# The third and fourth weight sums of a group are written over the loaded block that they are the last to read

## The chip, the cores and the metric

The kernel runs on one core of one Trainium2 chip. The metric is the device time of one execution in microseconds, taken as the median of repeated runs. TensorE (PE) does the matrix products, VectorE (DVE) and ScalarE (ACT) the element work, GpSimd (POOL) a little of it, and SyncE (SP) issues nearly all loads.

## The reference, cut to what matters

One decoder layer on 256 tokens of width 1024: three attention mixers, a gated merge, a layer norm, then a feed-forward part. The change lies in the second product of the feed-forward part, `w_down`, with 4096 rows of 1024:

```python
x = layer_norm(ALPHA * x + merged @ w_out[i], ln1_g[i], ln1_b[i])
h = jnp.square(jax.nn.relu(x @ w_up[i])) @ w_down[i]
ple = jax.nn.sigmoid(x @ w_ple_gate[i]) * (p[i] @ w_ple[i])
x = layer_norm(ALPHA * x + h + ple, ln2_g[i], ln2_b[i])
```

## The kernel before, in words

**A block and its split.** Weights come in blocks of 128 x 1024 fp32 (512 KB). `Weights._split` loads a block into a `raw` buffer (SP, L71), ACT casts it to a high part `whi` (L75), and DVE subtracts that to get the low part `wlo` (L79). TensorE then takes three products per tile, in `prod`: high by high (L133), with `wlo` (L134), and with the low part of the activations (L135). There are five `raw` buffers and five pairs of `whi` and `wlo`. A load waits on SP's queue until its `raw` buffer is free, that is until the last reader of the tile that held it has ended.

**The down product.** 16 of the 32 row blocks of `w_down` are multiplied plainly (here p1 to p16, read from `wdn`, 12 products of 512 columns each). The other 16 form four groups (`quad(u)`, QUADS = 4) by a scheme with seven products instead of eight. Each group loads three blocks a, c, d and a sum t1. The sum t1 is loaded into a tile called `rows` by a plain load from SP (L728) and a second load from POOL that adds to it (L729). From these DVE makes t2 = t1 + c, t3 = t2 - a and t4 = t2 + d in `make` (L752). All seven are split and multiplied like any block, with 6 products of 512 columns each. Here t4 of group 2 is called t4(2), and so on.

**Order.** TensorE takes the units in this order, which a loop writes out (three units of the groups, then a plain block):

```
a1 t1(1) c1 p1 | t2(1) t3(1) d1 p2 | t4(1) a2 t1(2) p3 | c2 t2(2) t3(2) p4 | d2 t4(2) a3 p5
t1(3) c3 t2(3) p6 | t3(3) d3 t4(3) p7 | a4 t1(4) c4 p8 | t2(4) t3(4) d4 p9 | t4(4) p10 ... p16
```

Each engine works through its own queue in a fixed order that a scheduler sets when the kernel is built. So on DVE the making of t2 stands in line with the splits, and a making of t2 whose c has not landed holds up every split behind it. Before, t2 has a buffer of its own (pool `p3`), and t3 and t4 each take one of the five `raw` buffers.

**The end.** The last six plain blocks go to five accumulators one after the other: b0, b4 and b1 (512 columns each), then b3 and b2 (256 each). As each is finished, DVE adds it to the rest (L833 before, L834 in the changed kernel), takes statistics (L605), and normalises (L617, L619). `rs` comes from POOL (L612).

Of the kernel before, what the change touches and what calls it, by code (L numbers as in the profile page):

```python
# [11 lines left out]
F32 = mybir.dt.float32  # L12
# [81 lines left out]
def hybrid_layer(ctx: ExitStack, tc: tile.TileContext, x0, xn, pT, wqk, wva, wvb, wg, wbc, wba,  # L94
# [5 lines left out]
    raw = ctx.enter_context(tc.tile_pool(name="raw", bufs=5))  # L100
# [26 lines left out]
    t = banks.tile([128, 512], F32, name="b4", tag="b4")  # L127
# [39 lines left out]
    for t in TASKS:  # L167
# [4 lines left out]
        elif t in "gcao":  # L172
            u, w, n = {"g": (u_g, wg, 1024), "c": (u_bc, wbc, 640), "a": (u_ba, wba, 768),
                       "o": (u_out, wout, 1024)}[t]
# [250 lines left out]
    for j in range(4):  # L425
# [3 lines left out]
        for h in range(2):  # L429
            act.activation(r[:, h], s[h], AF.Relu)  # L430
            for b in range(2):
                n = 2 * j + h
# [38 lines left out]
    for j in range(3):  # L471
# [5 lines left out]
        for h in range(2):  # L477
            n = 2 * j + h
# [9 lines left out]
    for j in range(3):  # L488
# [3 lines left out]
        for h in range(2):  # L492
            n = 2 * j + h
# [91 lines left out]
    p3 = ctx.enter_context(tc.tile_pool(name="p3", bufs=1, reuse_waits="tile"))  # L585
# [57 lines left out]
    for b in range(2):  # L643
        t = slice(b * 128, (b + 1) * 128)
# [31 lines left out]
    for f in range(32):  # L676
# [21 lines left out]
        if m % 2 == 0:  # L698
            continue
        hi, lo, y = ((hQ[:, u, 0, 0], hQ[:, u, 0, 1], g[:, 0, 0:2]) if m == 1 else  # L700
                     (hQ[:, u, 1:3, 0], hQ[:, u, 1:3, 1], g[:, :, 2:4]))
# [23 lines left out]
    def first_sum(u):  # L725

        if u < QUADS:
            nc.sync.dma_start(pair[:, u % 2], wdq[u, 1])  # L728
            pool.dma_start(pair[:, u % 2], wdq[u, 0], accum_op=ALU.add)  # L729
# [6 lines left out]
    def quad(u):  # L736

        t = {}

        def load(n):  # L740
            t[n] = raw.tile([128, 1024], F32, name="raw", tag="raw")
            nc.sync.dma_start(t[n], wdq[u, "abcd".index(n)])
            return t[n]

        def have():
            t["t1"] = pair[:, u % 2]
            return t["t1"]

        def make(n, x, y, f):
            p = p3 if n == "t2" else raw  # L750
            t[n] = p.tile([128, 1024], F32, name="raw", tag="raw")
            dve.tensor_tensor(t[n], t[x], t[y], op=f)  # L752
            if n == "t2":
                first_sum(u + 2)
            return t[n]

        A = [(hQ[:, u, m, 0], hQ[:, u, m, 1]) for m in range(3)]
        Z = sums[u]
        return [(lambda: load("a"), A[0], "P1"), (have, Z[0], "P5"),
                (lambda: load("c"), Z[3], "12"),  # L760
                (lambda: make("t2", "t1", "c", ALU.add), Z[1], "P6"),
                (lambda: make("t3", "t2", "a", ALU.subtract), Z[2], "P7"),
                (lambda: load("d"), A[1], "11"),
                (lambda: make("t4", "t2", "d", ALU.add), A[2], "21")]
# [189 lines left out]
```

## Time and profile before

| | |
|---|---|
| median of 3 runs | 448.35 us (447.51 to 448.59) |
| the profiled execution: time | 447.16 us |
| the profiled execution: span | 445.4 us |
| PE busy in the span | 428.7 us (96%) |
| DVE, ACT, POOL busy | 339.7, 272.7, 104.5 us |
| granted TensorE clock, mean | 0.996 |

The profile was taken on one execution; its own time is 1.8 us longer than the span of its instructions. A busy PE is not PE at its peak: products are pipelined, and each is shown from its start to its modelled end, so two in a row overlap. The distance from start to start says more.

### The profile page before, as it was taken

How to read it: one execution, taken by the hardware profiler on the slowest of the kernel's cores; microseconds unless marked ns; L12 is line 12 of the kernel's file. 1: busy time of each engine (PE TensorE's matmuls, PEld its weight loads, DVE VectorE, ACT ScalarE, POOL GpSimd, SP SyncE). 2: the span in 40 equal slices, each digit the busy share in tenths (PEclk: the TensorE clock that was granted, in tenths of full speed). 3: DMA queues.
4: the chain of work that ended last, by engine and by line, in shares of the span. 5: the costliest groups of instructions: out<-in, count | busy, mean ns of one | idle time of the engine just before them, and what ended most of it. 6: DMA issues, size and time to landing. Idle time of an engine off the chain costs nothing.

```text
span 445.4 us, 7749 instructions
## 1 busy us (share of the span) xinstructions
PE 428.7 (96%) x2833; PEld 386.8 (87%) x2833; DVE 339.7 (76%) x608; ACT 272.7 (61%) x491; POOL 104.5 (23%) x103
## 2 busy tenths in 40 slices
PE   7999999998999999999999999999999999899992
PEld 7989999998999989999886888888888888678882
DVE  4978977446545578759958779999987978779966
ACT  6765465576777748857605567778885865564600
POOL 2654256388533546500001000000000000000001
PEclk9999999999999999999999999999999999999998
DMA  8896855539634336459860866556793658457702
GB/s 290 297 325 181 255 176 182 157 114 302 204 110 141 125 88 198 135 175 330 278 242 1 294 211 192 190 185 203 248 282 115 164 188 237 148 182 243 277 0 95
DMA packets 27722, 86.38 MB, mean 194 GB/s; under 512 B 2928, under 2 KB 6936, under 8 KB 27300
## 3 DMA queue, kind: packets, MB, share of 16 engines
q1 hardware_dynamic: 25872, 79.54, 54.0%
q0 software_dynamic: 672, 2.16, 2.8%
q10 hardware_dynamic: 1140, 4.19, 2.7%
q8 instruction: 22, 0.36, 0.3%
q14 instruction: 16, 0.13, 0.1%
HBM read 83.98 MB, written 1.90 MB: 193 GB/s over the span
## 4 chain that ended last, share of the span: by engine, by line
PE 54%; DVE 8%; DMA 6%; issue 5%; ACT 1%; POOL 1%; POOLq 0%; DVEq 0%; SPq 0%
PE mm L681 10%; PE mm L133 7%; PE mm L134 7%; PE mm L135 7%; DMA raw<-in_wdq_dram 6%; PE b L134 5%; PE b L135 5%; PE mm L683 5%; PE b L133 5%; DVE wlo L79 4%; PE b L271 1%; DVE raw L752 1%; DVE r L686 1%; ACT whi L75 1%; DVE st L605 1%
## 5 line engine op out<-in xcount | busy, mean ns | idle before, releaser
L75 ACT CAST whi<-raw 128x1024 fp32r<-128x1024 f32 (+3 forms) x146 | 146.6, 1012 | 82.0 <-issue 17.9
L79 DVE TENSOR_TENSOR wlo<-raw,whi 128x1024 fp32r<-128x1024 f32 (+5 forms) x146 | 156.2, 1083 | 38.6 <-ACT whi L75 34.9
L79 POOL TENSOR_TENSOR wlo<-raw,whi 128x384 fp32r<-128x384 f32 (+3 forms) x58 | 76.5, 1325 | 84.8 <-ACT whi L75 72.9
L133 PE MATMUL mm<-xh,whi 128*128 128x256 f32 x336 | 95.0, 283 | 1.0 <-DVE G L251 1.0
L135 PE MATMUL mm<-xh,wlo 128*128 128x256 f32 x336 | 95.5, 284 | 0.0
L134 PE MATMUL mm<-xl,whi 128*128 128x256 f32 x336 | 94.7, 282 | 0.0
L133 PEld LDWEIGHTS mm<-xh,whi 128*128 128x128 f32 x336 | 63.3, 188 | 1.5 <-DVE G L251 1.2
L681 PE MATMUL mm<-x,whi 128*128 128x512 f32 x256 | 64.1, 392 | 0.0
L135 PEld LDWEIGHTS mm<-xh,wlo 128*128 128x128 f32 x336 | 63.3, 188 | 0.8
L134 PEld LDWEIGHTS mm<-xl,whi 128*128 128x128 f32 x336 | 63.3, 188 | 0.3
L681 PEld LDWEIGHTS mm<-x,whi 128*128 128x128 f32 x256 | 46.1, 189 | 8.3
L683 PEld LDWEIGHTS mm<-x,wlo 128*128 128x128 f32 x256 | 34.9, 190 | 2.5
L683 PE MATMUL mm<-x,wlo 128*128 128x256 f32 x256 | 35.7, 282 | 0.0
L729 POOL DMA_DIRECT2D rows<-in_wdq_dram x4 | 3.5, 880 | 131.4 <-DMA rows<-in_wdq_dram 131.4
L134 PE MATMUL b<-wlo,hT 128*128 128x512 f32 (+1 forms) x82 | 31.5, 385 | 1.9 <-DVE wlo L79 1.9
L135 PE MATMUL b<-whi,hT 128*128 128x512 f32 (+1 forms) x82 | 31.1, 380 | 0.0
L612 POOL TENSOR_TENSOR rs<-rs,half 128x1 f32<-128x1 f32 x4 | 4.1, 1030 | 111.4 <-DVE rs L611 111.4
L133 PE MATMUL b<-whi,hT 128*128 128x512 f32 (+1 forms) x82 | 27.5, 379 | 0.0
L686 DVE TENSOR_REDUCE r<-mm 128x256 f32<-128x512 f32 x32 | 22.0, 687 | 4.5 <-PE mm L683 4.5
L134 PEld LDWEIGHTS b<-wlo,hT 128*128 128x128 f32 x82 | 15.4, 188 | 6.3 <-DVE wlo L79 3.6
L687 ACT ACTIVATE r<-r 128x256 f32<-128x256 f32 x32 | 13.3, 416 | 10.0 <-DVE r L686 10.0
L134 PE MATMUL mm<-op,whi 128*128 128x256 f32 x64 | 18.0, 282 | 0.0
(198 smaller groups left out, 813.9 us busy)
## 6 DMA issues: line engine op xcount, KB each, us to landing
raw<-in_wup_dram SPq DMA_DIRECT2D x32, 512.0 KB
raw<-in_wg_dram SPq DMA_DIRECT2D x24, 512.0 KB
raw<-in_wqk_dram SPq DMA_DIRECT2D x18, 512.0 KB
raw<-in_wdn_dram SPq DMA_DIRECT2D x16, 512.0 KB
raw<-in_wdq_dram SPq DMA_DIRECT2D x12, 512.0 KB
raw<-in_wout_dram SPq DMA_DIRECT2D x8, 512.0 KB
raw<-in_wpg_dram SPq DMA_DIRECT2D x8, 512.0 KB
T<-tabd SPq DMA_DIRECT2D x24, 128.0 KB
```

The lines of the kernel that those rows point to most:

```text
L75: nc.scalar.copy(hi, r)
L79: e.tensor_tensor(lo[:, c], r[:, c], hi[:, c].bitcast(F32), op=ALU.subtract)
L133: pe.matmul(ps, lhsT=a[0], rhs=b[0], start=first, stop=False)
L134: pe.matmul(ps, lhsT=a[0], rhs=b[1], start=False, stop=False)
L135: pe.matmul(ps, lhsT=a[1], rhs=b[0], start=False, stop=last)
L271: m = pe.matmul(ss[h][:, QC[b]], lhsT=q[d, x, c], rhs=k[d, y, 0:128 * (b + 1)], start=i == 0, stop=i == 2)
L605: dve.bn_stats(st[b][:, c], y)
L681: pe.matmul(ps, lhsT=hi[:, cs[k]], rhs=x1[:, :, k], start=k == 0, stop=False)
L683: pe.matmul(ps[:, :, 0], lhsT=lo[:, cs[k]], rhs=x1[:, :, k, 0], start=False, stop=k == KT - 1)
L686: dve.tensor_reduce(r, ps.rearrange("p b a t -> p b t a"), axis=AX.X, op=ALU.add)
L687: act.activation(r, r, AF.Relu)
L752: dve.tensor_tensor(t[n], t[x], t[y], op=f)
```

## The change

In `make`, t3 and t4 no longer take a new `raw` buffer. The output is the tile `t[y]` that the sum is the last to read: t3 is written over a, t4 over d. Only t2 still gets a tile of its own, as before.

```diff
         def make(n, x, y, f):
-            p = p3 if n == "t2" else raw
-            t[n] = p.tile([128, 1024], F32, name="raw", tag="raw")
+            t[n] = t[y]
+            if n == "t2":
+                t[n] = p3.tile([128, 1024], F32, name="raw", tag="raw")
             dve.tensor_tensor(t[n], t[x], t[y], op=f)
```

The group stage now takes 28 `raw` buffers in turn instead of 36: eight sums no longer take one. t3 has to wait until a has been cast and split, t4 until d has been. The lines after this place move down by one (L752 is L753, L833 is L834). The number of instructions, loads and products is the same; what moves is which release each load waits for, and the order on DVE, ACT and PE.

By the semaphore counts in the two built programs, these loads wait for these instructions:

| load | before: waits for the end of | after: waits for the end of |
|---|---|---|
| d1 | the split of the last `w_up` block | the split of the `w_up` block before it |
| c2 | the split of d1 | the split of t3(1), which stands in a1's buffer |
| d2 | the making of t3(2) | the split of t4(1) |
| c3 | the split of p4 | the split of t3(2), which stands in a2's buffer |
| d3 | the making of t3(3) | the split of t4(2) |
| a4 | the split of p6 | the split of c3 |
| c4 | the split of t3(3) | the split of p6 |

First place: DVE's queue at the seam of groups 2 and 3, before. In the names, raw_4657 is d2, raw_4669 t4(2), raw_4721 c3, raw_4733 t2(3), raw_4681 a3, raw_4763 t3(3), raw_4693 p5, and rows_4458 t1.

```order
L79 TENSOR_TENSOR wlo_4660<-raw_4657,whi_4659 128x1024
L79 TENSOR_TENSOR wlo_4672<-raw_4669,whi_4671 128x1024
L752 TENSOR_TENSOR raw_4733<-rows_4458,raw_4721 128x1024
L79 TENSOR_TENSOR wlo_4684<-raw_4681,whi_4683 128x1024
L752 TENSOR_TENSOR raw_4763<-raw_4733,raw_4681 128x1024
L79 TENSOR_TENSOR wlo_4696<-raw_4693,whi_4695 128x1024
L79 TENSOR_TENSOR wlo_4712<-rows_4458,whi_4711 128x1024
```

The same place after. Here raw_4654 is d2 and then t4(2), raw_4717 c3, raw_4729 t2(3), raw_4677 a3 and then t3(3), raw_4689 p5.

```order
L79 TENSOR_TENSOR wlo_4657<-raw_4654,whi_4656 128x1024
L753 TENSOR_TENSOR raw_4654<-raw_4611,raw_4654 128x1024
L753 TENSOR_TENSOR raw_4729<-rows_4458,raw_4717 128x1024
L79 TENSOR_TENSOR wlo_4668<-raw_4654,whi_4667 128x1024
L79 TENSOR_TENSOR wlo_4680<-raw_4677,whi_4679 128x1024
L79 TENSOR_TENSOR wlo_4692<-raw_4689,whi_4691 128x1024
L753 TENSOR_TENSOR raw_4677<-raw_4729,raw_4677 128x1024
```

The making of t4(2) moved from earlier in the queue to behind d2's split, and t4(2)'s split now stands behind the making of t2(3), where it stood ahead of it.

Second place: PE's queue shortly before the accumulators b0, b4, b1 are finished, before. b3_5026 is accumulator b3.

```order
L133 MATMUL b1_4539<-whi_4991,hT_2959 128x512
L133 MATMUL b3_5026<-whi_4949,hT_2959 128x256
L134 MATMUL b3_5026<-wlo_4950,hT_2959 128x256
L135 MATMUL b3_5026<-whi_4949,hT_2959 128x256
L134 MATMUL b0_4532<-wlo_4992,hT_2959 128x512
```

The same place after (b3_5018 is b3; the L133 and L134 of its first block stand further up).

```order
L133 MATMUL b1_4538<-whi_4983,hT_2959 128x512
L135 MATMUL b3_5018<-whi_4941,hT_2959 128x256
L133 MATMUL b3_5018<-whi_4953,hT_2959 128x256
L134 MATMUL b3_5018<-wlo_4954,hT_2959 128x256
L135 MATMUL b3_5018<-whi_4953,hT_2959 128x256
L134 MATMUL b0_4531<-wlo_4984,hT_2959 128x512
```

Six products of b3 now stand ahead of the last ones of b0, b4 and b1; before there were three.

Third place: DVE's queue in the final normalisation, before.

```order
L605 BN_STATS st_5100<-Y_3172 128x6
L619 SCALAR_TENSOR_TENSOR Y_3172<-Y_3172,rs_5071,rows_5015 128x512
L833 TENSOR_TENSOR Y_3172<-b3_5026,PL_2960 128x256
L619 SCALAR_TENSOR_TENSOR Y_3172<-Y_3172,rs_5071,rows_5015 128x512
L833 TENSOR_TENSOR Y_3172<-b2_5027,PL_2960 128x256
L605 BN_STATS st_5100<-Y_3172 128x6 x2
```

The same place after.

```order
L605 BN_STATS st_5092<-Y_3172 128x6
L834 TENSOR_TENSOR Y_3172<-b3_5018,PL_2960 128x256
L619 SCALAR_TENSOR_TENSOR Y_3172<-Y_3172,rs_5063,rows_5007 128x512 x2
L605 BN_STATS st_5092<-Y_3172 128x6
L834 TENSOR_TENSOR Y_3172<-b2_5019,PL_2960 128x256
L605 BN_STATS st_5092<-Y_3172 128x6
```

The last statistics now stand directly behind the add that they read; before, another statistics instruction stood between.

## The prediction

> **What bounds the kernel now.** First the page: busy times, the slices, and the chain that ended last.
>
> ```profile
> span 445.4 us, 7749 instructions
> PE 428.7 (96%) x2833; PEld 386.8 (87%) x2833; DVE 339.7 (76%) x608; ACT 272.7 (61%) x491; POOL 104.5 (23%) x103
> PE 54%; DVE 8%; DMA 6%; issue 5%; ACT 1%; POOL 1%; POOLq 0%; DVEq 0%; SPq 0%
> PE mm L681 10%; PE mm L133 7%; PE mm L134 7%; PE mm L135 7%; DMA raw<-in_wdq_dram 6%; PE b L134 5%; PE b L135 5%; PE mm L683 5%; PE b L133 5%; DVE wlo L79 4%; PE b L271 1%; DVE raw L752 1%; DVE r L686 1%; ACT whi L75 1%; DVE st L605 1%
> ```
>
> TensorE is the bound, yet 6% of the chain, some 27 us, are loads of the groups' blocks. A share of the chain is no loss: while such a load is awaited TensorE may still have split blocks in stock. So I next asked for the busy time by stretch of the group stage, and for who waits there (columns of the waits: us in total, times, longest).
>
> ```profile
> 351.00:382.00 31.00, 31.00 (x142) 25.75 (x141) 23.45 (x23) 19.53 (x24) 1.71 (x2) 1.00 0.70 204
> 382.00:404.00 22.00, 20.05 (x85) 15.36 (x84) 19.11 (x18) 11.19 (x11) 0.00 (x0) 1.00 0.46 147
> 404.00:428.00 24.00, 24.00 (x109) 19.94 (x108) 22.22 (x24) 12.61 (x13) 0.00 (x0) 1.00 0.60 216
> PE b L134 <- DVE wlo L79: 1.9, 3, 0.8
> DVE raw L752 <- DMA raw<-in_wdq_dram: 12.0, 5, 4.3
> ```
>
> TensorE (second number, after the length) is full in the first and third stretch at a clock of 1.00, and idle only between 382 and 404, for 22.00 - 20.05 = 1.95 us. It waits there for splits, and the splits stand behind makings of t2 that wait for c: 12.0 us of waiting on DVE end as 1.95 us on TensorE. The timeline of TensorE shows the holes.
>
> ```profile
> 380.38 0.39 PE L134 MATMUL b<-wlo,hT 128*128 128x512 f32 x1
> 380.61 0.39 PE L135 MATMUL b<-whi,hT 128*128 128x512 f32 x1
> ...
> 382.42 0.39 PE L133 MATMUL mm<-whi,hT 128*128 128x512 f32 x1
> 383.65 0.50 PE L134 MATMUL b<-wlo,hT 128*128 128x512 f32 x1 [0.84 <-DVE wlo L79]
> 383.99 0.40 PE L135 MATMUL b<-whi,hT 128*128 128x512 f32 x1
> ...
> 384.92 0.39 PE L133 MATMUL b<-whi,q 128*128 128x512 f32 x1
> 385.92 0.50 PE L134 MATMUL b<-wlo,hT 128*128 128x512 f32 x1 [0.62 <-DVE wlo L79]
> 386.26 0.40 PE L135 MATMUL b<-whi,hT 128*128 128x512 f32 x1
> ...
> 399.47 0.39 PE L133 MATMUL b<-whi,hT 128*128 128x512 f32 x1
> 400.35 0.50 PE L134 MATMUL b<-wlo,hT 128*128 128x512 f32 x1 [0.49 <-DVE wlo L79]
> 400.69 0.40 PE L135 MATMUL b<-whi,hT 128*128 128x512 f32 x1
> ...
> 402.32 0.39 PE L133 MATMUL b<-whi,q 128*128 128x512 f32 x1
> 402.62 0.50 PE L134 MATMUL b<-wlo,hT 128*128 128x512 f32 x1
> 402.95 0.40 PE L135 MATMUL b<-whi,hT 128*128 128x512 f32 x1
> ```
>
> Undisturbed products start 0.23 us apart (380.38, 380.61). Measured by starts, the holes cost more than the idle time shows: 383.65 - 382.42 - 0.23 = 1.00, 385.92 - 384.92 - 0.23 = 0.77, 400.35 - 399.47 - 0.23 = 0.65 and 402.62 - 402.32 - 0.23 = 0.07, and after each the next start comes 0.33 to 0.34 on instead of 0.23, 0.11 more, four times. Together 2.49 + 0.43 = 2.92 us. The four are the first uses of the low parts of a3, p5, p7 and a4: each stands on DVE behind t2(3) or t2(4). The chain of waits, DVE's timeline and ACT's give the times behind them.
>
> ```profile
> 357.49 5.37 DMA raw<-in_wdq_dram
> 366.54 3.38 DMA raw<-in_wdq_dram
> 374.68 6.44 DMA raw<-in_wdq_dram
> 393.17 4.63 DMA raw<-in_wdq_dram
> 354.98 2.48 DVE L79 TENSOR_TENSOR wlo<-raw,whi 128x1024 fp32r<-128x1024 f32 x2 [0.24 <-ACT whi L75]
> 371.16 5.76 DVE L79 TENSOR_TENSOR wlo<-raw,whi 128x1024 fp32r<-128x1024 f32 x5
> 381.24 1.23 DVE L752 TENSOR_TENSOR raw<-rows,raw 128x1024 f32<-128x1024 f32 x1 [4.32 <-DMA raw<-in_wdq_dram]
> 382.38 1.22 DVE L79 TENSOR_TENSOR wlo<-raw,whi 128x1024 fp32r<-128x1024 f32 x1
> 368.38 1.05 ACT L75 CAST whi<-raw 128x1024 fp32r<-128x1024 f32 x1 [0.53 <-PE b L135]
> 372.19 1.05 ACT L75 CAST whi<-raw 128x1024 fp32r<-128x1024 f32 x1 [0.76 <-PE mm L135]
> DMA to landing us min/median/max: 5.5/7.9/11.1
> ```
>
> The four loads are c2, d2, c3 and c4. They land after 3.38 us at best and 6.44 at worst. c3 could be issued only at 374.68, when the third of five splits in a row (p4) had freed its buffer. The last line is the accumulating load of t1 from POOL, whose four issues land after 5.5 to 11.1 us. The casts are those of t3(2), at 368.38, and of d2, at 372.19.
>
> **The change, part by part.** Nothing is added or taken away on TensorE, and every load, cast, split and sum stays. Counted by starts, a DVE instruction of this kind takes 382.38 - 381.24 = 1.14 us.
>
> *Loads released earlier.* c2 waits for the first of the two splits at 354.98 instead of the second: 1.14 us earlier, 356.3, and with 5.37 us it lands at 361.7 instead of 362.9. c3 now waits for the split of t3(2). Its cast ends at 368.38 + 1.05 = 369.4, still bound by TensorE giving a pair of split buffers back, so the split ends at about 369.5 + 1.22 = 370.7, and c3 is issued there, 4.0 us earlier. In the kernel before, that split came after t4(2), which waited for d2 (366.54 + 3.38 = 369.92). d2 is now released by t4(1)'s split, near 364, so that wait goes too. d1's earlier load and the later t3(1) in the last products of `w_up` I cost at nothing: no row shows TensorE waiting there. The cover is the stock of split blocks. If it were gone, t3(1) would cost its 1.14 us.
>
> *The new place in DVE's queue.* t4(2) waits for d2's split: cast 372.19 + 1.05 = 373.2, split to 374.5, t4(2) to 375.7. On ACT its cast then stands until about 375.8, with the casts of a3 and p5 queued behind it; they end by 378.8, ahead of the splits that need them. Behind t4(2) on DVE stands t2(3), and behind that now the split of t4(2), then those of a3 and p5. TensorE wants t4(2)'s low part at 380.38 (the first row of its timeline above). That part is there 1.14 + 1.22 = 2.4 us after c3 has landed, so c3 may land at 378.0. With the latencies of the four loads it lands at 374.1 (3.38) to 377.1 (6.44), and there is no hole. But it now leaves SP within a microsecond or two of the accumulating load for t1(4), which moves up as well, since it follows t1(2)'s split. With that load's median of 7.9 us as c3's latency, c3 lands at 378.6, the low part is there at 381.0, and the hole is 0.6 + 0.11 = 0.7 us. I take this value, because the shared transfer is the nearest row for such a neighbour; the ends are 0 and, with 11.1 us (381.8, low part at 384.2), 3.9 us.
>
> The Trainium skill, "DMA: Bandwidth & Descriptors", section "Anatomy of one DMA — SWDGE (gpsimd) path", fits a transfer on that path as about 2.0 us plus its bytes at 436 GB/s; for 512 KB that makes an estimate of 3.2 us. The trace agrees for a load alone (3.38) and not for one among others (5.37, 6.44). By the page the new hole would be 0 and the sum below 445.9.
>
> *Group 4.* From t2(3)'s start, about 378.7, the split of p6, which now releases c4, is the eighth after it: eight steps of 1.14 and 1.22 give 389.0, against 393.17. With c4's 4.63 us it lands at 393.7, and t4(3)'s low part is there at 396.1. TensorE would want it, without the first two holes, near 395.5 to 396.2. I take 0 here; 0.6 at most is inside the bounds above. p7 and a4 follow one step later each, against 1.36 us of products (6 x 0.23) in each unit, and have no hole.
>
> *The end.* Two rows of TensorE and four of DVE price it.
>
> ```profile
> 432.59 0.28 PE L133 MATMUL b<-whi,hT 128*128 128x256 f32 x1
> 432.71 0.28 PE L134 MATMUL b<-wlo,hT 128*128 128x256 f32 x1
> 429.17 0.69 DVE L833 TENSOR_TENSOR Y<-b,PL 128x512 f32<-128x512 f32 x1 [2.79 <-PE b L135]
> 429.89 0.70 DVE L605 BATCH_NORM_STATS2 st<-Y 128x6 f32<-128x512 f32 x1
> 432.80 0.69 DVE L833 TENSOR_TENSOR Y<-b,PL 128x512 f32<-128x512 f32 x1 [0.15 <-PE b L135]
> 439.81 1.42 DVE L619 SCALAR_TENSOR_TENSOR Y<-Y,rs,rows 128x640 f32<-128x640 f32 x2
> ```
>
> From the add at 432.80 to the last normalising at 439.81 DVE runs on and sets the end. That add is released by b1, and three more products of b3 stand ahead of it: 3 x 0.12 = 0.36 us later against the same amount of TensorE work. The last statistics now follow the add that they read: a dependent instruction starts 0.03 us after the end (429.17 + 0.69 against 429.89), an independent one 0.09 before it (381.24 + 1.23 against 382.38), so 0.12 us. Bounds: 0, if DVE finds a gap after all, and 0.48.
>
> *Sum.* -2.92 + 0.7 + 0.36 + 0.12 = -1.74 us. Against the profiled execution's 447.16 us (span 445.4 and 1.8 around it) that is 445.4. That execution lies 1.19 below the median of the runs, 448.35, from which I count: **446.6 us**. With the holes gone TensorE itself is late next, and nothing in this stage can give more.
>
> **The rivals.** *The loads win nothing (no measurable change).* The holes go, but c3, p5, a3 and the accumulating load run together earlier instead of later, and a hole of 2 to 3 us opens at t4(2), or at t4(3) as well: -2.92 + 2.5 + 0.48 = 0.06, 448.4 us. For it: t4(2)'s split was ahead of t2(3) and is now behind it, so the same lateness of c3 hits a unit that TensorE wants 2 to 3 us sooner; and the shared loads took 5.37 and 6.44 us. Against: c3 starts 4.0 us earlier, more than that. The Trainium skill, "Trainium Kernel Development and Optimization", section "Key Constraints", says that loads from SP, ACT and POOL interleave on the same 16 engines; 6.44 against 3.38 us fits it.
>
> *Slower.* The same place, with c3 slower still. It decides from a hole of 2.92 - 0.48 + 1.35 = 3.8 us, when t4(2)'s low part comes at 384.2 and c3 lands at 381.8, 11.1 us after its issue: the longest of the four accumulating loads. That gives 449.7 us. Against it: no plain load on the chain took over 6.44.
>
> *The change doesn't do what it says.* DVE's own work, not the buffers, would set the holes: 19.11 us busy of 22 between 382 and 404. Then TensorE keeps about its 2.92 us, and the end adds 0.48: 448.8. Against: DVE waited 4.32 us in one piece for c3 just ahead of the first hole.
>
> **How the numbers follow.** This kernel's runs can tell about 0.3%, 1.35 us, from no change. My forecast, holes gone but for 0 to 1 us: 0.57, 445.9 to 446.9 (its own range). Loads win nothing: 0.30, 447.5 to 448.6. Doesn't do what it says: 0.06, 448.8. Slower: 0.07, 449.7. The forecast counts as faster but for 0.04 of its upper end, which lies close to 447.0. So faster 0.53, same 0.04 + 0.30 + 0.06 = 0.40, slower 0.07. The range: from 445.7 (no new hole, 448.35 - 2.92 + 0.48 = 445.9, less 0.2 for the spread of runs, 447.51 to 448.59) to 448.6 (the second case's upper end) leaves out the slower case and half of the one before.
>
> **What would show it.** Right: no TensorE hole behind t2(3) or t2(4); c3 issued near 370.7; the wait of t2(3) far below 4.32 us; at the start of t4(2)'s second product a hole of at most 0.8 us; the last gapless DVE run beginning 0.36 us nearer to TensorE's end. Wrong: a wait for `wlo` of 2 us or more at t4(2), an accumulating load that lands later than before relative to c3, or holes that stay behind a3 and p5.

## The result, and the profile after

| | before | after |
|---|---|---|
| median | 448.05 us (6 runs, 446.90 to 448.59) | 445.62 us (6 runs, 443.77 to 446.06) |
| profiled execution: time, span | 447.16, 445.4 us | 445.60, 443.8 us |

The ratio of after to before is 0.9939, 95% interval 0.9916 to 0.9962: faster by 2.4 us in the medians and by 1.56 us between the two profiled executions, where 1.74 was forecast. The ratios here and below are not those of the medians, which would give 0.9946 here. Two executions of the later experiments that took 606.0 us (e10) and 707.95 us (e12), at a granted clock of 0.66 and 0.56 against 0.99, are left out of medians and ratios. The median lies 1.0 us below the predicted 446.6 and 0.08 below the low end of the range.

The page after: span, busy times, and the chain by engine.

```profile
span 443.8 us, 7749 instructions
PE 428.8 (97%) x2833; PEld 388.1 (87%) x2833; DVE 338.6 (76%) x608; ACT 272.9 (61%) x491; POOL 106.5 (24%) x103
PE 81%; DVE 6%; DMA 5%; issue 3%; ACT 2%; POOL 2%; SPq 0%; POOLq 0%; DVEq 0%
```

TensorE's busy time is what it was (428.7), and the span is 1.6 us shorter. The same three stretches of the group stage, and the two waits:

```profile
351.00:382.00 31.00, 30.64 (x140) 25.21 (x139) 24.96 (x25) 20.37 (x24) 1.71 (x2) 1.00 0.74 204
382.00:404.00 22.00, 22.00 (x98) 18.20 (x98) 21.38 (x19) 12.70 (x14) 0.00 (x0) 1.00 0.69 222
404.00:428.00 24.00, 24.00 (x110) 19.96 (x109) 19.61 (x23) 10.39 (x11) 0.00 (x0) 1.00 0.44 148
PE b L134 <- DVE wlo L79: 0.4, 1, 0.4
DVE raw L753 <- DMA raw<-in_wdq_dram: 7.2, 4, 2.9
```

The stretch from 382 to 404, which had 1.95 us of idle TensorE, is full. DVE still waits 7.2 us for the four loads of c (11.6 before; 0.4 of the 12.0 was for d3), and one wait of TensorE is left, 0.36 us just before 382. The timeline of DVE, POOL, SP and TensorE there, with the first product of `w_up` on top (it serves as the zero from which the group stage is timed below):

```profile
262.88 1.30 PE L681 MATMUL mm<-x,whi 128*128 128x512 f32 x5
370.25 0.86 POOL L729 DMA_DIRECT2D rows<-in_wdq_dram  x1 [17.59 <-DMA rows<-in_wdq_dram]
371.64 0.33 SPq L742 DMA_DIRECT2D raw<-in_wdq_dram  x1
379.39 1.23 DVE L753 TENSOR_TENSOR raw<-rows,raw 128x1024 f32<-128x1024 f32 x1 [2.95 <-DMA raw<-in_wdq_dram]
380.53 3.49 DVE L79 TENSOR_TENSOR wlo<-raw,whi 128x1024 fp32r<-128x1024 f32 x3
380.83 0.61 PE L133 MATMUL b<-whi,hT 128*128 128x512 f32 x2
381.81 0.50 PE L134 MATMUL b<-wlo,hT 128*128 128x512 f32 x1 [0.36 <-DVE wlo L79]
382.14 0.40 PE L135 MATMUL b<-whi,hT 128*128 128x512 f32 x1
393.81 1.23 DVE L753 TENSOR_TENSOR raw<-rows,raw 128x1024 f32<-128x1024 f32 x1 [0.59 <-DMA raw<-in_wdq_dram]
```

c3 is issued at 371.64. t2(3) starts at 379.39, t4(2)'s split right behind it, and TensorE gets that low part at 381.81. The two products at 380.83 are 0.23 apart, so the hole is 381.81 - 381.06 - 0.23 = 0.52, with 0.11 more at the next start 0.63 us. It is the only one: by starts the holes fell from 2.92 to 0.63 us. The chain of waits has c2's load and c3's, issue and time to landing:

```profile
356.37 4.81 DMA raw<-in_wdq_dram
371.64 7.62 DMA raw<-in_wdq_dram
```

And the end, TensorE's last product and DVE ("last product" below is the start of TensorE's last instruction):

```profile
431.43 0.69 DVE L834 TENSOR_TENSOR Y<-b,PL 128x512 f32<-128x512 f32 x1 [0.15 <-PE b L135]
434.70 0.28 PE L135 MATMUL b<-x,hT 128*128 128x256 f32 x1
436.00 0.41 DVE L834 TENSOR_TENSOR Y<-b,PL 128x256 f32<-128x256 f32 x1
436.44 0.43 DVE L605 BATCH_NORM_STATS2 st<-Y 128x6 f32<-128x256 f32 x1
438.57 1.41 DVE L619 SCALAR_TENSOR_TENSOR Y<-Y,rs,rows 128x640 f32<-128x640 f32 x2
```

b1's add now starts 434.70 - 431.43 = 3.27 us before TensorE's last product starts; before it was 3.63. From that add to DVE's end it is 8.55 us against 8.43.

The span, cut at those points, in each of the two executions:

| stretch | before | after | difference |
|---|---|---|---|
| start to the first `w_up` product | 262.21 | 262.88 | +0.67 |
| `w_up` | 89.24 | 89.24 | 0 |
| last `w_up` product to the last product | 84.98 | 82.57 | -2.41 |
| last product to DVE's end | 4.80 | 5.29 | +0.49 |
| DVE's end to the end of the span | 4.15 | 3.82 | -0.33 |

The change acts in the third and fourth rows, -1.92 us together. Why the last row is 0.33 us shorter no run shows. The first row differs between executions of one and the same program: three profiled executions of the changed kernel have 262.88, 262.33 and 261.03.

### The profile page after: what moved, and what is told of

Its sections match the earlier page's. It is cut to its first block, busy times and chain, and to the rows that moved or that the text cites. A ratio compares the mean times of both kernels' runs of the same rounds, so it can differ in the third digit from the quotient of the medians.

```text
span 443.8 us, 7749 instructions
## 1 busy us (share of the span) xinstructions
PE 428.8 (97%) x2833; PEld 388.1 (87%) x2833; DVE 338.6 (76%) x608; ACT 272.9 (61%) x491; POOL 106.5 (24%) x103
## 4 chain that ended last, share of the span: by engine, by line
PE 81%; DVE 6%; DMA 5%; issue 3%; ACT 2%; POOL 2%; SPq 0%; POOLq 0%; DVEq 0%
PE mm L681 13%; PE mm L133 11%; PE mm L135 11%; PE mm L134 11%; PE mm L683 7%; PE b L135 6%; PE b L134 6%; PE b L133 6%; PE b L271 3%; PE b L409 3%; DMA raw<-in_wdq_dram 3%; DVE wlo L79 2%; DMA T<-tabd 1%; ACT whi L75 1%; DMA pr<-in_pT_dram 1%
## 5 line engine op out<-in xcount | busy, mean ns | idle before, releaser
L79 POOL TENSOR_TENSOR wlo<-raw,whi 128x384 fp32r<-128x384 f32 (+3 forms) x58 | 78.5, 1358 | 83.3 <-ACT whi L75 72.2
L133 PE MATMUL mm<-xh,whi 128*128 128x256 f32 x336 | 95.0, 283 | 1.0 <-DVE G L251 1.0
L134 PE MATMUL mm<-xl,whi 128*128 128x256 f32 x336 | 94.7, 282 | 0.0
L133 PEld LDWEIGHTS mm<-xh,whi 128*128 128x128 f32 x336 | 63.3, 188 | 1.5 <-DVE G L251 1.2
L134 PEld LDWEIGHTS mm<-xl,whi 128*128 128x128 f32 x336 | 63.3, 188 | 0.3
L134 PE MATMUL b<-wlo,hT 128*128 128x512 f32 (+1 forms) x82 | 31.0, 380 | 0.4 <-DVE wlo L79 0.4
L133 PE MATMUL b<-whi,hT 128*128 128x512 f32 (+1 forms) x82 | 27.4, 379 | 0.0
L134 PEld LDWEIGHTS b<-wlo,hT 128*128 128x128 f32 x82 | 15.4, 188 | 3.7 <-DVE wlo L79 0.8
L133 PEld LDWEIGHTS b<-whi,hT 128*128 128x128 f32 x82 | 15.4, 188 | 3.0
```

What stands on the lines that cost most here:

```text
L79: e.tensor_tensor(lo[:, c], r[:, c], hi[:, c].bitcast(F32), op=ALU.subtract)
L133: pe.matmul(ps, lhsT=a[0], rhs=b[0], start=first, stop=False)
L134: pe.matmul(ps, lhsT=a[0], rhs=b[1], start=False, stop=False)
```

## The experiments

The question after the result was why c3, issued earlier by 3 us and more, still left a hole, and what sets that hole's size. Theory: c3's transfer runs behind the accumulating load of t1 that POOL issues a moment before, so c3's landing hangs on that load, not on the freed buffer; and t4(2)'s split, now behind the making of t2(3), hands every delay of c3 to TensorE. Rivals: the buffers alone set it; t3's place or t4's place does it alone; or the gain is spread of the runs. "Before" is each time the kernel before on the same chip: median 447.22 us in the first four experiments (26 runs), 446.49 in the next four (30), 446.68 in the last four (29).

**The change again, e1 and e11.** No edit.

> The changed kernel once more, to settle its size. Theory (the holes): TensorE's holes in the group stage, 2.92 us before, are 0.63 us in the changed kernel's trace, and the end costs 0.48 us more, so 1.8 us less than before, ratio 0.996, in every run that has this one hole at t4(2). Rival (something else also got faster): the ratio stays at 0.994 or lower, 2.4 us or more, and a trace shows a stretch outside 380 to 437 us that is shorter.

> The changed kernel a third time. Theory (one hole at t4(2), whose size goes with c3's landing; the rest as before): a hole of 0.5 to 1.4 us there and nowhere else, ratio 0.995 to 0.998. Rival (the gain is spread of runs): ratio 0.998 to 1.002.

e1: 445.25 us (12 runs), ratio 0.9985 (0.996 to 1.001), a hole of 0.82 at the same place. Taken alone, e1 cannot tell the change from none: three of its 12 runs took 447.3 us or more, though its median is 2.0 us below before. e11: 445.41 us (12 runs), ratio 0.9957 (0.9937 to 0.9978), and in its profile no hole at all, where 0.5 to 1.4 was expected. The three comparisons of the change, the narrower interval weighing more, give 0.9959 together, or 1.8 us. Two of the three intervals exclude no change, so the gain is real; the first one's 2.4 us overstates it. The size of the hole differs from execution to execution. The timeline of e11:

```profile
261.03 1.98 PE L681 MATMUL mm<-x,whi 128*128 128x512 f32 x8
367.25 0.86 POOL L729 DMA_DIRECT2D rows<-in_wdq_dram  x1 [17.75 <-DMA rows<-in_wdq_dram]
369.55 0.33 SPq L742 DMA_DIRECT2D raw<-in_wdq_dram  x1
376.19 1.23 DVE L753 TENSOR_TENSOR raw<-rows,raw 128x1024 f32<-128x1024 f32 x1 [1.60 <-DMA raw<-in_wdq_dram]
```

From the first `w_up` product, t2(3) starts at 376.19 - 261.03 = 115.16 here and at 379.39 - 262.88 = 116.51 in the first profile. The accumulating load, seen from the same zero, went out at 106.22 here and at 107.37 there.

**One half of the change, e2 and e9 (t3 alone), e3 and e10 (t4 alone).**

```diff
-            if n == "t2":
-                t[n] = p3.tile([128, 1024], F32, name="raw", tag="raw")
+            if n != "t3":       # e3, e10: n != "t4"
+                p = p3 if n == "t2" else raw
+                t[n] = p.tile([128, 1024], F32, name="raw", tag="raw")
```

> Only t3 is written over a; t4 takes a raw buffer again. Theory: c2 is released by t3(1)'s split, but t4 again takes a buffer from the loads, so c3 and c4 gain about half of what they gain in the full change; holes of 1 to 2 us are left, at a3, p5 or p7 rather than at t4(2), and the time lies 1.0 to 1.8 us below before. Rival (t3 alone carries the gain): one hole of at most 0.7 us, and the time of the full change, 2.4 us below before.

> Only t3 is written over a; t4 takes a raw buffer. The first profile of this order had 3.25 us of holes on TensorE, yet its median was 0.996 of the kernel before. Theory (the holes are those of late c loads, and one execution with a stretch of half clock and late loads is not typical): the profile now shows 0.5 to 2 us of holes, and the ratio is again 0.995 to 0.998. Rival (t3 alone brings nothing to the group stage, and what the median gained comes from elsewhere): holes of 3 us or more again.

> Only t4 is written over d; t3 takes a raw buffer again. Theory: the hole at t4(2) is 0.6 to 1.7 us, since t4's split stands behind the making of t2(3) as in the full change and c3 is released later; 0.8 to 1.8 us below before. Rival (t4 alone carries the gain): the time of the full change, 2.4 us below before. Rival (the new place in the queue costs more than the buffer brings): no faster than before, a hole of 2 us or more.

> Only t4 is written over d; t3 takes a raw buffer. Theory (t4 over d is the half that removes the holes): no hole over 0.3 us in the group stage, ratio 0.993 to 0.996, that is 1.8 to 3.1 us below the kernel before. Rival (the first profile was a lucky execution): holes of 1 us or more, ratio 0.996 to 1.

t3 alone: 444.88 us, ratio 0.996 (0.9935 to 0.9985), and again 445.66 us, 0.9969 (0.9949 to 0.999). e2's profile is of its longest execution, 449.09 us, with holes of 3.25 us and a stretch of half clock at 28.5 us, far from the group stage; e9's has 1.00 us of holes, as the theory there said. t4 alone: 445.27 us, 0.9954 (0.9935 to 0.9973), and again 446.38 us (11 runs), 0.9994 (0.9967 to 1.0021). e3's profile has no hole, where 0.6 to 1.7 us was expected; e10's has one of 2.13 us, so its rival, that the first profile was a lucky execution, was right. t3 alone gains in both comparisons. t4 alone gains in one, and in the other nothing that can be told from zero. The runs do not tell the halves apart.

The two profiles of one program, e3 and e10, tell more than the medians. First e3:

```profile
372.51 0.33 SPq L742 DMA_DIRECT2D raw<-in_wdq_dram  x1
372.67 0.86 POOL L729 DMA_DIRECT2D rows<-in_wdq_dram  x1 [18.73 <-DMA rows<-in_wdq_dram]
377.66 1.22 DVE L754 TENSOR_TENSOR raw<-rows,raw 128x1024 f32<-128x1024 f32 x1 [1.13 <-DMA raw<-in_wdq_dram]
```

Then e10, with TensorE and the window at the end:

```profile
371.24 0.86 POOL L729 DMA_DIRECT2D rows<-in_wdq_dram  x1 [18.25 <-DMA rows<-in_wdq_dram]
371.95 0.33 SPq L742 DMA_DIRECT2D raw<-in_wdq_dram  x1
380.58 1.23 DVE L754 TENSOR_TENSOR raw<-rows,raw 128x1024 f32<-128x1024 f32 x1 [4.45 <-DMA raw<-in_wdq_dram]
380.52 0.61 PE L133 MATMUL b<-whi,hT 128*128 128x512 f32 x2
382.99 0.50 PE L134 MATMUL b<-wlo,hT 128*128 128x512 f32 x1 [1.85 <-DVE wlo L79]
384.03 0.63 PE L135 MATMUL b<-whi,hT 128*128 128x512 f32 x1
384.46 1.48 PE L133 MATMUL b<-whi,hT 128*128 128x512 f32 x3
384.00:387.40 3.40, 3.40 (x9) 2.64 (x8) 3.40 (x5) 1.05 (x1) 0.00 (x0) 0.50 0.30 70
```

In e3 c3 goes out 0.16 us ahead of the accumulating load and lands 5.0 us later. In e10 it goes out 0.71 us behind it and takes 8.5. The order of instructions is the same. Counted from the first `w_up` product (262.98 and 262.57), c3's issue differs by 0.15 us (109.53 and 109.38), and t2(3)'s start by 3.3 (114.68 and 118.01). The rows of TensorE show what the hole cost in this execution besides itself: after 1.85 us of idling the clock falls to half at 384.0 (0.50 in the window), and for 3.4 us the products start 0.43 us apart (384.03, 384.46) instead of 0.23, eight of them 0.20 later, 1.6 us on top of the hole's 2.13.

**Without the accumulating load, e7.** This kernel leaves out the second half of t1, that is the addition from POOL.

```diff
-            pool.dma_start(pair[:, u % 2], wdq[u, 0], accum_op=ALU.add)
```

> The full change without the second, accumulating load of t1 in every group (t1 is then only its first half, so this part of the sum is left out). Theory (the accumulating load makes c3 late): c3 lands 3.3 to 4.8 us after its issue instead of 7.6 us, the making of t2(3) waits under 1 us, the hole at t4(2) is gone, and the time is 0.6 us below the full change. Rival (c3 is late for its place in the queue of loads alone): it still takes over 6 us and the hole of 0.63 us stays.

444.52 us, ratio 0.9952 (0.9934 to 0.997), no hole. DVE no longer waits for c3 there (no wait stands in the row, from DVE's timeline):

```profile
376.19 1.22 DVE L752 TENSOR_TENSOR raw<-rows,raw 128x1024 f32<-128x1024 f32 x1
```

c3 was issued at 371.11 in it and had landed by 376.19, so it took at most 5.1 us. With the accumulating load gone, c3 is no longer slow. This takes away the addition and its 512 KB of traffic at once; no run tells which of the two delays c3.

**c first, e4.** From the second group on, c is loaded and multiplied ahead of a and t1.

```diff
-        return [(lambda: load("a"), A[0], "P1"), (have, Z[0], "P5"),
-                (lambda: load("c"), Z[3], "12"),
+        first = [(lambda: load("a"), A[0], "P1"), (have, Z[0], "P5"), (lambda: load("c"), Z[3], "12")]
+        return (first if u == 0 else [first[2], first[0], first[1]]) + [
```

> The full change, and in groups 2 to 4 the order of the first three units is c, a, t1 instead of a, t1, c, so that c is loaded two loads earlier. Theory: c3 is issued some 3 us or more ahead of 371.6, the making of t2(3) waits under 1 us, and the last hole at t4(2), 0.63 us, is gone: 0.6 us less than the full change. If c's lateness were no cause of the hole, it stays at 0.6 us and so does the time.

442.97 us (6 runs), ratio 0.9913 (0.9894 to 0.9932); the interval lies below that of e1, which ran beside it. The windows and DVE's row for t2(3):

```profile
351.00:382.00 31.00, 31.00 (x142) 25.82 (x141) 28.19 (x28) 20.58 (x26) 1.71 (x2) 1.00 0.81 222
382.00:404.00 22.00, 22.00 (x99) 18.22 (x98) 20.21 (x18) 13.50 (x14) 0.00 (x0) 1.00 0.69 224
377.08 1.22 DVE L753 TENSOR_TENSOR raw<-rows,raw 128x1024 f32<-128x1024 f32 x1
```

TensorE is full and t2(3) waits for nothing. Here c3 goes out ahead of the plain and the accumulating load of t1, with the same loads, buffers and sums. The last product starts 81.88 us after `w_up`'s last, against 82.57: 0.69 us less, where the theory had 0.63. The medians of e4 and e1 differ by 2.3 us, and the hole is not all of it. In e4's profile DVE also ends 4.67 us after the last product instead of 5.29, and b1's add, at 430.81, starts 3.75 us before that product (at 434.56) instead of 3.27: the order at the end changed too.

**The end in the old order, e5, and with c first, e6.** The products for b3 and b2 are kept behind the last of b1.

```diff
+            with ExitStack() as held:
+                if b == 1 and c > 0:
+                    held.enter_context(tc.issue_after(done_b1[0]))
```

> The full change, and the products of b3 and b2 may not be moved ahead of b1's last product on TensorE. Theory (from the add of b1 on, DVE sets the end): b1 is finished six products of 0.12 us sooner against TensorE's end, so the add of b1 starts 4.0 us instead of 3.27 us before TensorE's last product, and the time is 0.7 us below the full change. Rival (TensorE's end sets it, through b2): no change.

> The full change with c first in groups 2 to 4 and with b3 and b2 kept behind b1. Theory: both terms add, 0.63 + 0.72 = 1.35 us below the full change, no hole in the group stage. Rival: less than 0.7 us below it, because the one takes the place of the other.

e5: 444.63 us (12 runs), ratio 0.9955 (0.9932 to 0.9978). Its timeline at the end:

```profile
430.58 0.69 DVE L834 TENSOR_TENSOR Y<-b,PL 128x512 f32<-128x512 f32 x1
434.57 0.28 PE L135 MATMUL b<-x,hT 128*128 128x256 f32 x1
437.85 1.41 DVE L619 SCALAR_TENSOR_TENSOR Y<-Y,rs,rows 128x640 f32<-128x640 f32 x2
```

b1's add starts 3.99 us before TensorE's last product, and DVE ends 4.69 after it instead of 5.29: the 0.48 us that the change costs at the end come back, with 0.1 more. The time does not show the 0.7 us that was expected: 0.9955 against 0.9959 for the change. Its profile had a hole of 1.33 us, which would hide it, but one profile cannot tell that for the other 11 runs. e6: 443.21 us (7 runs), ratio 0.9928 (0.9902 to 0.9954), no hole, span 441.4. It isn't told apart from e4; both are ahead of the change and of the kernel before.

**Fewer and more buffers, e8 and e12.** e8 is the changed kernel with four `raw` buffers; e12 is the kernel before with six. To make room, e12 takes the square behind `w_up` in place; the edit is in the `w_up` loop, right ahead of the group stage, and not in the attention, as the expectation has it.

```diff
-    raw = ctx.enter_context(tc.tile_pool(name="raw", bufs=5))
+    raw = ctx.enter_context(tc.tile_pool(name="raw", bufs=4))     # e12: bufs=6
...                                                                # e12 alone:
-            q = w2.tile([128, S], F32, name="q2", tag="q2")
-            act.activation(q, r.rearrange("p b t -> p (b t)"), AF.Square)
+            q = r.rearrange("p b t -> p (b t)")
+            act.activation(q, q, AF.Square)
```

> The full change with four raw buffers instead of five, in the whole kernel. Theory (the number of buffers that loads find free sets the holes): the holes of the group stage come back, 2 to 3.5 us in all, and the time is 2 us or more above the full change, about that of before. Rival (the holes come from the order on DVE, not from the buffers): 0.7 us of holes as with five, and no change in that stage.

> The kernel before with six raw buffers instead of five; room for the sixth comes from squaring an activation in place (the attention's square, early in the program). t3 and t4 take buffers as before. Theory (what counts is that loads find a buffer earlier, not where t3 and t4 are written): c2 and c3 go out at least 2 us earlier against TensorE than before, the holes shrink from 2.9 us to under 1, and the group stage from the last w_up product to the last product falls from 84.98 to 82 to 83 us. Rival (it is the new order of DVE's queue that the change brings): the group stage stays at 84.5 us or more. The schedule of the earlier stages also moves, so the stage's length is read from the profile rather than from the total.

e8: 449.62 us, ratio 1.0073 (1.0046 to 1.0099); a hole of 2.84 us at t4(2), as its theory said, and again half clock behind it, from 383.6 to 387.0. The time was expected near that of before and is 3.1 us above it. e12: 451.36 us (5 runs), ratio 1.0103 (1.0074 to 1.0133). Of e12's loss 4.2 us lie ahead of `w_up` (its first product starts at 266.42), where the schedule moved too; its group stage, from `w_up`'s last product, takes 84.33 us, which seems to lie between the two theories. But two products of that stage (2 x 0.23 us) already run before `w_up`'s last product there, and `w_up` takes 89.69 us instead of 89.24. Counted from the first `w_up` product, the last product starts at 174.02 us in e12, 174.22 before and 171.81 after. Six buffers win 0.2 us where the change wins 2.4, so the theory failed and the rival's number came out. Its reason is not shown: DVE's queue is not the one of before in e12 either. Its holes, by starts, are still 2.78 us in all, 1.88 of them at t4(2), whose split stands behind t2(3) here as after the change. Its window and the largest wait:

```profile
382.00:404.00 22.00, 20.33 (x88) 15.93 (x87) 17.92 (x16) 11.60 (x11) 0.00 (x0) 1.00 0.47 156
386.60 0.50 PE L134 MATMUL b<-wlo,hT 128*128 128x512 f32 x1 [1.61 <-DVE wlo L79]
```

c2 goes out 93.39 us after the first `w_up` product, as early as after the change (93.49; 95.28 before). c3 goes out at 110.81, 1.7 earlier than before but 2.1 later than after, and waits for the accumulating load all the same. With 36 turns on six buffers there are 6.0 for each, with 28 on five 5.6, before it was 7.2.

**What sets the hole.** From the profiles with t4(2)'s split behind t2(3), read like those above (c3's landing is 0.13 us before t2(3) where no chain has it), and three others for the transfers alone:

| profile | c3's issue behind POOL's | c3, issue to landing | POOL's issue to c3's landing | t2(3) after first `w_up` product | hole, without its 0.11 |
|---|---|---|---|---|---|
| e3 | -0.16 | 5.0 | 4.9 | 114.68 | 0 |
| e10 | 0.71 | 8.5 | 9.2 | 118.01 | 2.02 |
| e1 | 1.33 | 7.1 | 8.4 | 116.69 | 0.71 |
| after | 1.39 | 7.6 | 9.0 | 116.51 | 0.52 |
| e5 | 1.93 | 6.3 | 8.3 | 117.21 | 1.22 |
| e12 | 2.00 | 6.8 | 8.8 | 117.76 | 1.77 |
| e11 | 2.30 | 6.5 | 8.8 | 115.16 | 0 |
| e8 | 2.99 | 7.7 | 10.7 | 118.71 | 2.73 |
| before | 2.45 | 6.4 | 8.9 | 119.03 | (other order) |
| e2 | 4.09 | 5.2 | 9.3 | 119.08 | (other order) |
| e9 | 4.24 | 4.7 | 8.9 | 117.33 | (other order) |

Two things can be read from it. The hole is t2(3)'s start less 115.98 us in every row, to 0.01, and 0 where that is negative: DVE hands c3's delay on without loss. And wherever c3 goes out behind the accumulating load, it lands 8.3 to 9.3 us after that load's issue (10.7 in e8), though it left between 0.71 and 4.24 us behind it. In each of these profiles c3 landed after the accumulating load had, by 0.2 to 2.7 us.

## Why the prediction was right and where it failed

- *The four holes, -2.92.* All four are gone in the three profiles of the change. This step held.
- *The new hole at t4(2), 0.7, ends 0 and 3.9.* 0.63, 0.82 and 0 in three profiles. Place and cause were right. That the first one came within 0.07 us is luck: against the first `w_up` product c3 left 0.27 us later than forecast and took 7.62 us instead of 7.9, the low part came 0.14 us later than forecast, and TensorE wanted it 0.24 us, about one product, later. c3's latency was 7.1 and 6.5 us in the other two. The prediction's "load alone" (d2, 3.38 us) was not alone: the plain half of t1(4) left SP 1.10 us behind it, at 367.64. Both are loads from SP, while the fit set beside them is for POOL's path, whose four loads took 5.5 to 11.1 us.
- *c3 issued 4.0 us earlier, at 370.7.* 371.64, in an execution that began the stage 0.67 later. Against the first `w_up` product it is 108.76 instead of 112.47, 3.7 earlier. But t2(3) moved only from 119.03 to 116.51, by 2.5: the accumulating load moved by 2.65 (from 372.23 - 262.21 = 110.02 to 107.37), and c3's landing went with that load. The prediction named it as c3's neighbour, and did not see that c3 lands behind it. One of its signs of being wrong did show, without harm: the accumulating load landed 1.9 us ahead of c3 before and 0.3 after. The row of before:

```profile
372.23 0.86 POOL L729 DMA_DIRECT2D rows<-in_wdq_dram  x1 [19.82 <-DMA rows<-in_wdq_dram]
```

- *c2 issued at 356.3, landing at 361.7; c4 landing at 393.7, no hole in group 4.* 356.37 and 361.18, in an execution 0.67 later, so c2 left 1.8 us earlier and not 1.14; t2(4) starts at 393.81; no hole. t2(3)'s wait, called "far below 4.32", is 2.95.
- *d1 and t3(1) at nothing.* `w_up` takes 89.24 us in both, and no hole opens behind it.
- *The end, 0.36 + 0.12.* 3.63 - 3.27 = 0.36 and 8.55 - 8.43 = 0.12. Both to the hundredth.
- *The sum, -1.74.* -1.92 where the change acts, -1.56 in the profiled pair, about -1.8 over three comparisons. The 2.4 us between the first medians is more than any of these.

**The step that failed is the low end of the range**: "no new hole, 448.35 - 2.92 + 0.48 = 445.9, less 0.2 for the spread of runs". The 0.2 was mis-sized. The kernel before, over the 85 runs of the three later sessions, went from 444.40 to 449.74 us, and its medians of some 30 runs lie at 447.22, 446.49 and 446.68; the 448.35 of three runs, from which the forecast counted, is 1.1 to 1.9 above them. The changed kernel's three medians, 445.62, 445.25 and 445.41, agree far better. A base from three runs needed, by this estimate, about 1.5 us either way, not 0.2. Counted from the three later medians, the same sum gives 445.5, 444.8 and 444.9 us with low ends of 444.6, 443.9 and 444.0, and all three medians of the changed kernel lie above those. So the mechanism held and the base was off. In the first comparison the median lay 0.99 us below the sum: 0.30 because the base was 448.05 with six runs, 0.69 because the difference was 2.43 instead of 1.74. What spreads is seen in the profiles: the start stage (261.0 to 264.1 us in the five-buffer kernels of the table and e2), the hole, which the same program shows with 0 or 2 us, and a stretch of half clock in some executions.

Of the rivals, *the loads win nothing* (a new hole of 2 to 3 us) came true in single executions: 2.13 us in e10, where only t4 was moved. *Slower* put its deciding point at a hole of 3.8 us. It came sooner in one execution: e10 with 2.13 us has a group stage of 85.65 us, longer than the 84.98 before, because the half clock adds 1.6 us there. No profile of the change itself shows it. *DVE's own work sets the holes* is out: in e4 DVE does the same work and TensorE is full.

## What to carry to other kernels

Freeing a buffer earlier lets a load leave earlier; whether it lands earlier depends on what stands in front of it on the transfer side, so follow every early load to its landing beside its neighbours. A work item placed in a queue behind a consumer of a late load inherits the whole delay: here sending c ahead of the accumulating load (e4) removed the last hole, 0.7 us in the group stage on top of the freed buffers, while six buffers (e12) won 0.2 us. Judge a change of half a per cent from many runs of both kernels beside each other, and add the terms of a prediction to a base that has as many.

## What the runs showed of the hardware

- A 512 KB load issued 0.7 to 1.4 us behind an accumulating load of the same size took 7.1 to 8.5 us to land, 0.16 us ahead of it 5.0 us, and without it (e7) at most 5.1. Issued 4.1 to 4.2 us behind it (e2, e9), it took 4.7 to 5.2.
- TensorE's granted clock fell to half after idling of 1.85 us (e10) and 2.57 us (e8), 0.9 to 1.0 us after the products had started again, and came back after 3.4 us. The length of the gap alone does not decide it: in e12 the clock stayed at 1.00 after gaps of 1.86 and 1.90 us, and in e2 it fell at 28.48 us for 3.4 us with no gap over 0.50 us in the 3.4 us before. The rows of e8 and, last, of e12, with the idle time in brackets and the clock third from the end of a window's row:

```profile
382.70 0.50 PE L134 MATMUL b<-wlo,hT 128*128 128x512 f32 x1 [2.57 <-DVE wlo L79]
383.60:387.00 3.40, 3.40 (x10) 2.62 (x9) 3.40 (x4) 1.04 (x1) 0.00 (x0) 0.50 0.78 202
216.19 1.15 PE L133 MATMUL mm<-whi,ph 128*128 128x512 f32 x3 [1.90 <-ACT whi L75]
211.69:215.10 3.41, 2.14 (x8) 1.42 (x8) 3.41 (x5) 2.62 (x6) 0.00 (x0) 1.00 0.79 279
215.10:218.52 3.42, 2.33 (x9) 1.62 (x10) 3.42 (x6) 2.09 (x5) 0.00 (x0) 1.00 0.83 281
```

What fits e10, e8 and e12 is where a gap lies. In all 14 profiles every change of the granted clock comes a whole number of steps of 3.4133 us after its first rise (e10 and e8: 378.88 us, 111 steps; e2: 23.89 us, 7 steps). In the step that ends with the fall TensorE was idle for 1.85 us in e10 and 2.55 us in e8. In no other step before the last product of any profile was it idle for more than 1.52 us; each of e12's two gaps falls on two steps (for the one of 1.90 us the last two rows, with 1.27 and 1.09 us idle). The step before e2's fall has only 0.50 us of idling, but many small products (36x384, 64x128, 128x328), so idle time is not all that counts.

The Trainium skill, "TensorE: Matmul & The Clock Gate", section "HAM oscillation — how this bites in real kernels", puts the limit for idle gaps of TensorE at about 3.4 us. The length of the half-clock stretch here agrees with that number, the limit does not: gaps of 1.85 and 2.57 us were enough. By that rule e10's hole would have cost 2.13 us; it cost about 3.7. Three falls in 14 profiles are few, so the steps are shown and what in a step sets the limit stays open.
